# Modulation tiles of the first feed-forward stage in a ring of their own, and half-chunk steps

## The chip, the cores and the metric

The kernel runs on one core of one Trainium2 chip. The metric is the device time of one execution in microseconds (us); the median of three runs is given.

## The reference, cut to what matters

Two layers of a diffusion backbone work on two token streams of 256 tokens each (a latent and a context stream, D = 1024). Each layer is: a half-step SwiGLU feed-forward, a mixer of four branches (latent attention, Hyena convolution, S5 state space, neighbourhood attention), and a second half-step feed-forward. Each of these is wrapped in norms with shift, scale and gate vectors that come from the conditioning vectors:

```python
mod_l = (act_l @ w_mod[i] + b_mod[i])          # 9 vectors of 1024 for the latent stream
mod_c = (act_c @ w_mod[i][:, :n_c] + b_mod[i][:n_c])   # the same weights, context
def ffn_sublayer(x, mods, base, g_pre, g_post, w_in, w_out):
    h = rms_norm(x, g_pre) * (1 + mods[base + 1]) + mods[base]
    a, b = jnp.split(h @ w_in, 2, axis=-1)     # 1024 -> 2 x 2816
    return x + 0.5 * mods[base + 2] * rms_norm((silu(a) * b) @ w_out, g_post)
```

Vectors 0 to 2 belong to the first feed-forward, 3 to 5 to the mixer, 6 to 8 to the second feed-forward. The S5 parameters are turned into tables of powers, and the Hyena filters are computed by a small network with sines and a transform; neither depends on the tokens.

## The kernel before, in words

All large products run on TensorE (PE) in three passes of fp32r halves (hi x hi, hi x lo, lo x hi). A weight chunk of 128 x 1024 comes by a DMA of the SP queue into one of four slots of the tag `raw`, ACT makes its upper half `wh` (L220) and DVE its lower half `wl` (L221). The feed-forward (`ffn`) walks over 22 chunks f of 128 hidden columns; a chunk is two units (the a and the b half), each of 24 matmuls of 512 columns at full streams (L227 to L229, into one of four PSUM banks). `gate` forms silu(a) * b in a tile `t` (two slots) and splits it into `gg` (L541 to L548). The `gg` tiles of chunks 0 to 7, 8 to 15 and 16 to 21 lie in three pools. The output projection follows with 16 weight chunks, and then six more.

Side work is emitted in small steps. After each chunk `ffn` calls `step(2)`, and after each of the 16 weight chunks of the output projection `step(1)`. A `stepper` skips its first calls and then hands out tiles in proportion to the weights. A modulation tile (`mod_flow`, 128 x 1024 of `w_mod`, vector j, piece k) is summed with a fused DVE instruction for one stream (L328), and for the other by a product on GpSimd (POOL, L332) and a sum on ACT in the following step (L306). For layer 0 and j of 5 or more both streams are summed on DVE. For layer 1 and j of 5 or more there is one stream, and its pieces go to DVE and POOL in turn.

The first feed-forward of layer 0 (`ffn(0, 0, ...)`, called at L800) has three kinds of side work: the S5 setup (`setup_s5`, on POOL and DVE, emitted ahead of `ffn` with a lower priority; its memory is later that of the `gg` tiles of chunks 8 to 15, so these wait for its stores), the Hyena filters (`hyena_filters`, one step per call, closed at chunk 16), and vectors 2 to 8 of layer 0, whose tiles are loaded by SP into `raw` (L298). They begin after six calls. The second feed-forward of layer 0 (L815 to L832) computes vectors 0 to 4 of layer 1, and the first of layer 1 (called at L848) vectors 5 to 8; in these two the tiles have a ring of two slots, are loaded by POOL's queue, and POOL also computes S5 tables for layer 1 (`s5_tables` by way of `ahead`; PE transposes them at L1206 and multiplies them at L1217).

The order of PE's instructions is as written. On the other engines, and on the DMA queues, a planner with its own timeline sets the order when the program is built; `after(...)` puts an instruction behind a named one of the same engine.

Of the kernel before, what the change touches and what calls it, by code (L numbers as in the profile page):

```python
# [9 lines left out]
F32 = mybir.dt.float32  # L10
# [153 lines left out]
def build(tc, A):  # L164
# [20 lines left out]
    with st, tc.manual_schedule(engines={mybir.EngineType.PE}):  # L185
# [99 lines left out]
        def mod_flow(l, js, act, raw=None):  # L285

            if callable(act):
                act = act()  # L290
            tiles = [(j, k) for j in js for k in range(KT)]
            ws, back = {}, []

            def load(n):
                if n < len(tiles):
                    j, k = tiles[n]
                    ws[n] = raw() if raw else rp.tile([P, D], F32, tag="raw", name="raw")
                    (G.dma_start if raw else dma)(ws[n], A["wmod"][l, j, k])  # L298

            def finish():  # L300
                while back:
                    back.pop(0)()

            def sums(w, s, c):
                with after(mark["wh"]):
                    S.activation(w, w, AF.Copy, scale=0.5, accum_out=md[l][:, s, c : c + 1])  # L306

            def bias(j, ss):
                for s in ss:
                    m = md[l][:, s, j * KT : (j + 1) * KT]  # L310
                    V.tensor_tensor(m, m, bmt[l][:, j * KT : (j + 1) * KT], op=ALU.add)

            if raw:
                load(0)
                yield
            for n, (j, k) in enumerate(tiles):
                finish()
                load(n + 1 if raw else n)
                c = j * KT + k
                w = ws.pop(n)  # L320
                ss = [1] if l == 1 and j >= 5 else [0, 1]
                both = l == 0 and j >= JB
                fast = ss if both else [] if ss == [1] and k % 2 else [1]
                slow = [s for s in ss if s not in fast]
                for s in fast:
                    jk = sp.tile([P, D], BF16, tag="sq", name="jk", bufs=1)
                    with after(mark["wl"]):
                        V.scalar_tensor_tensor(  # L328
                            jk, w, 0.5, act[s], op0=ALU.mult, op1=ALU.mult, accum_out=md[l][:, s, c : c + 1]
                        )  # L330
                for s in slow:
                    G.tensor_tensor(w, w, act[s], op=ALU.mult)  # L332
                    back.append(lambda w=w, s=s, c=c: sums(w, s, c))
                if k == KT - 1:
                    back.append(lambda j=j, ss=ss: bias(j, ss))
                yield
            finish()

# [194 lines left out]
        def ffn(l, i, h, late, toks, nxt, gp, step, rows, fill, begun=(), xpool2=None):  # L533
            g = []
            begun = list(begun)
            cs_all = slice(min(toks) * P, NTOK)

            def new_unit(f, ab):
                return begun.pop(0) if begun else unit(l, i, h, f, ab, cs_all)

            def gate(f, ps):  # L541
                t = sp.tile([P, 512], F32, tag="t", name="t")
                S.activation(t[:, cs_all], ps[0][:, cs_all], AF.Tanh, scale=0.5)
                V.scalar_tensor_tensor(t[:, cs_all], t[:, cs_all], 1.0, ps[0][:, cs_all], op0=ALU.add, op1=ALU.mult)
                V.scalar_tensor_tensor(t[:, cs_all], t[:, cs_all], 0.5, ps[1][:, cs_all], op0=ALU.mult, op1=ALU.mult)
                gg = gp(f // 8).tile([P, 2, 512], F32R, tag="gg", name="gg", bufs=min(8, NF - f // 8 * 8))
                split(gg[:, 0, cs_all], gg[:, 1, cs_all], t[:, cs_all])
                g.append((gg[:, 0], gg[:, 1]))  # L548

            for f in range(NF):  # L550
                u = [new_unit(f, ab) for ab in range(2)]
                if late and f == 0:
                    u2 = [new_unit(1, ab) for ab in range(2)]
                    pss = []

                    def keep(v):
                        def run(cs):
                            ps = v(cs)
                            if cs is CTX:
                                pss.append(ps)  # L560
                                if len(pss) == 2:
                                    gate(0, pss)

                        return run

                    front([keep(u[0]), keep(u[1]), keep(u2[0])], late)
                elif late and f == 1:
                    gate(1, [pss[2], u2[1](None)])
                else:
                    gate(f, [v(None) for v in u])  # L570
                step(2)
                if f == NF - 3:
                    nxt["gr"] = rows()

            def lhs(kt, m):
                ms = slice(m * P, (m + 1) * P)
                return g[kt][0][:, ms], g[kt][1][:, ms]

            n_ = [0]

            def place():
                n_[0] += 1
                return gp((n_[0] - 1) // 8).tile([P, 2, 512], F32R, tag="gg", name="wf", bufs=8).rearrange("p a b -> p (a b)")

            fill()
            return outproj(lhs, NF, A["foa"][l, i], A["fob"][l, i], toks, nxt, xpool2 or (lambda: gp(3)), place, step)
# [18 lines left out]
        def ahead(stack, gp, name, slices):  # L605

            gp(0)
            gp(1)
            ts = ExitStack()
            tq = ts.enter_context(tc.tile_pool(name=name, bufs=1, reuse_waits="tile"))  # L610
            gen = s5_tables(E, L - 1, slices, tabd, sds, tq, lambda: psy.tile([P, 512], F32, tag="py", name="pn"))

            def close():
                for _ in gen:
                    pass
                ts.close()

            gp.before[2] = close
            f, n = [0], 4 * len(slices) + 3

            def go():
                f[0] += 1
                for _ in range(n * f[0] // 15 - n * (f[0] - 1) // 15):
                    next(gen, None)

            return go
# [35 lines left out]
        with ExitStack() as fs:  # L662
# [99 lines left out]
                    f()  # L762
            nxt = {}
            gp = Gates(fs, "A")
            gp(0)
            with ExitStack() as s1:
                tp5 = pool(s1, "s5s")
# [22 lines left out]
                        acts.extend(act_load())  # L790
                return acts

            st0 = stepper([(mod_flow(0, [2, 3, 4], acts0), 25), (mod_flow(0, [5, 6, 7, 8], acts0), 33)], 46, 6)

            def step0(w):
                st0(w)
                with after(mark["sp"], mark["dve"]):
                    next(hyg, None)

            late = ffn(0, 0, h, late, TALL, nxt, gp, step0, lambda: gate_rows(0, 0, 1, 0.5, [0, 1]), fill0, begun)  # L800
            h = nxt["h"]

        E = dict(locals())
        for l in range(L):
# [8 lines left out]
            with ExitStack() as fs:  # L813
# [4 lines left out]
                else:  # L818
# [3 lines left out]
                        n3.update(coeff=pre_coeff(1, 0, 0, [0, 1]), h=new_h())  # L822

                    x1, raw1 = mod_ring(fs, "mrB")
                    st1 = stepper([(mod_flow(1, [0, 1, 2, 3, 4], act_load, raw1), 42)], 50, 2)
                    tg1 = ahead(fs, gp, "s5p", range(0, 3))

                    def step1(w):
# [5 lines left out]
            if not last:  # L834
                with ExitStack() as fs:
# [4 lines left out]
                        n4.update(coeff=pre_coeff(1, 3, 2, [0, 1]), h=new_h())  # L840

                    x2, raw2 = mod_ring(fs, "mrC")
                    st2 = stepper([(mod_flow(1, [5, 6, 7, 8], act_load, raw2), 34)], 50, 2)
                    tg2 = ahead(fs, gp, "s5q", range(3, 8))

                    def step2(w):
# [44 lines left out]
def hyena_filters(tc, A, hp, psy, Hd, dma, cp, sp, rp, split):  # L891
# [12 lines left out]
    for l in range(L):  # L904
# [19 lines left out]
        for i, w in enumerate((w1, w2)):  # L924
            ps = psy.tile([P, 512], F32, tag="py", name="psm")
            T.matmul(ps[:64, :256], lhsT=w, rhs=cur, start=True, stop=True)
            a = hp.tile([64, 256], F32, tag="a", name="a")
            n = hp.tile([64, 256], F32, tag="n", name="n")
            V.tensor_scalar(
                a, ps[:64, :256], hv[:, 2 * i : 2 * i + 1], hv[:, 2 * i + 1 : 2 * i + 2], op0=ALU.add, op1=ALU.mult  # L930
            )
# [10 lines left out]
        for nt in range(2):  # L942
            f12 = []
            for j in range(2):
                ps = psy.tile([P, 512], F32, tag="py", name="psm")
                c = slice(nt * P, (nt + 1) * P)
                js = slice(j * 512, (j + 1) * 512)
                T.matmul(ps, lhsT=c2[:, c], rhs=w3[:, js], start=True, stop=False)
                T.matmul(ps, lhsT=c2[:, c], rhs=w3l[:, js], start=False, stop=True)
                f = hp.tile([P, 512], F32, tag="f12", name="f12", bufs=2)  # L950
                V.tensor_tensor(f, ps, dec[:, nt], op=ALU.mult)
                f12.append(f)
            pair = []
            for op in (ALU.add, ALU.subtract):
                su = hp.tile([P, 512], F32, tag="su", name="su", bufs=1)
                V.tensor_tensor(su, f12[0], f12[1], op=op)
                if nt == 0 and op == ALU.add:
                    V.tensor_tensor(su[0:1], su[0:1], hyd, op=ALU.add)
# [7 lines left out]
        for ri in range(2):  # L966
            for kt in range(2):
                ps = psy.tile([P, 512], F32, tag="py", name="psm")
                for nt in range(2):
                    c = slice(kt * P, (kt + 1) * P)  # L970
                    for i, (a, b) in enumerate(((0, 0), (0, 1), (1, 0))):
# [4 lines left out]
                            start=nt == 0 and i == 0,  # L976
                            stop=nt == 1 and i == 2,
                        )
                H = hp.tile([P, 512], F32, tag="f12", name="H", bufs=2)
                S.activation(H, ps, AF.Copy)  # L980
                dma(Hd[l][:, ri * 2 + kt], H)
            if ri == 0:
# [1252 lines left out]
```

## Time and profile before

| | us |
|---|---|
| median of three runs | 2654.64 (2652.17 to 2656.76) |
| the profiled execution | 2656.14 |
| its span | 2654.4 |
| PE busy in it | 2499.3 (94%) |
| DVE, ACT, POOL busy | 1719.9, 1096.1, 819.0 |

Times in the rows below are us from the start of the span unless marked ns. Engines: PE is TensorE's matmul, DVE VectorE, ACT ScalarE, POOL GpSimd, SP the engine that issues most DMAs; "SPq" is its queue. "L227" is line 227 of the kernel. PEclk is the granted TensorE clock as a share of full speed.

### The profile page before, as it was taken

The numbers are of one execution on the slowest core, as the hardware profiler recorded it, in microseconds if no ns is written. First come the engines' busy times: TensorE is split into PE (matmuls) and PEld (weight loads), VectorE is DVE, ScalarE is ACT, GpSimd is POOL, SyncE is SP. The second block draws the span as 40 slices with busy tenths as digits, with TensorE's granted clock in tenths as the row PEclk, the third lists the DMA queues.
The fourth block names the chain that finished last, engine by engine and source line by source line (L and its number), as shares of the span: only waits on it lengthen the run. The fifth ranks groups of instructions, "written<-read, shape, count | busy, mean of one in ns | idle before, by whom it ended". The sixth has DMA issues, their size and how long they took to land. (4 is left out here: it accounts for less than half of the span.)

```text
span 2654.4 us, 38042 instructions
## 1 busy us (share of the span) xinstructions
PE 2499.3 (94%) x14606; PEld 2107.5 (79%) x14606; DVE 1719.9 (65%) x2544; ACT 1096.1 (41%) x1860; POOL 819.0 (31%) x844
## 2 busy tenths in 40 slices
PE   6978999999999889999899998799999999998998
PEld 3856788987788767887778887677888989997997
DVE  6788995555645898556887546564535567776564
ACT  5435323454543232444444334333324555445443
POOL 4884000100102774006975406884201011100000
PEclk8989999999999999999999999999999999999999
DMA  6345675222232233344565544655542335776564
GB/s 238 104 151 197 214 249 195 84 75 84 74 111 71 85 94 104 94 166 161 179 194 185 205 142 141 198 185 187 175 158 76 92 100 189 282 247 212 160 191 143
DMA packets 134209, 411.06 MB, mean 155 GB/s; under 512 B 27095, under 2 KB 39176, under 8 KB 131212
## 3 DMA queue, kind: packets, MB, share of 16 engines
q1 hardware_dynamic: 117388, 349.33, 40.4%
q0 software_dynamic: 16640, 59.31, 6.4%
q8 instruction: 115, 1.88, 0.3%
q14 instruction: 66, 0.54, 0.1%
HBM read 374.41 MB, written 34.16 MB: 154 GB/s over the span
## 5 line engine op out<-in xcount | busy, mean ns | idle before, releaser
L221 DVE TENSOR_TENSOR wl<-raw,wh 128x1024 fp32r<-128x1024 f32 x424 | 565.3, 1334 | 537.0 <-ACT wh L220 529.8
L220 ACT ACTIVATE wh<-raw 128x1024 fp32r<-128x1024 f32 x424 | 449.2, 1060 | 846.9 <-issue 253.8
L227 PE MATMUL pin<-hh,wh 128*128 128x512 f32 (+1 forms) x1468 | 535.9, 365 | 20.3 <-ACT wh L220 12.4
L229 PE MATMUL pin<-hh,wl 128*128 128x512 f32 (+1 forms) x1468 | 531.5, 362 | 15.4 <-DVE wl L221 15.3
L228 PE MATMUL pin<-hl,wh 128*128 128x512 f32 (+1 forms) x1468 | 531.9, 362 | 1.7 <-DVE hl L415 1.6
L246 POOL TENSOR_TENSOR r<-v,mhalf 128x1 f32<-128x1 f32 (+2 forms) x46 | 30.7, 667 | 1015.2 <-DVE v L245 916.5
L227 PEld LDWEIGHTS pin<-hh,wh 128*128 128x128 f32 x1468 | 284.9, 194 | 66.8 <-ACT wh L220 15.3
L229 PEld LDWEIGHTS pin<-hh,wl 128*128 128x128 f32 x1468 | 284.2, 194 | 60.0 <-DVE wl L221 19.1
L228 PEld LDWEIGHTS pin<-hl,wh 128*128 128x128 f32 x1468 | 284.4, 194 | 43.2 <-DVE hl L415 3.3
L1322 PE MATMUL pm<-hh,wh 128*128 128x512 f32 (+1 forms) x704 | 251.3, 357 | 0.0
L1324 PE MATMUL pm<-hh,wl 128*128 128x512 f32 (+1 forms) x704 | 245.0, 348 | 0.2 <-DVE wl L221 0.2
L1323 PE MATMUL pm<-hl,wh 128*128 128x512 f32 (+1 forms) x704 | 244.9, 348 | 0.0
L458 PE MATMUL y<-wh,gg 128*128 128x512 f32 x448 | 177.2, 396 | 0.0
L459 PE MATMUL y<-wl,gg 128*128 128x512 f32 x448 | 177.2, 396 | 0.0
L460 PE MATMUL y<-wh,gg 128*128 128x512 f32 x448 | 177.2, 396 | 0.0
L332 POOL TENSOR_TENSOR mraw<-mraw,act 128x1024 f32<-128x1024 f32 x56 | 141.2, 2522 | 57.8 <-DMA mraw<-wmod 28.2
L1322 PEld LDWEIGHTS pm<-hh,wh 128*128 128x128 f32 x704 | 134.0, 190 | 18.1 <-issue 2.5
L1324 PEld LDWEIGHTS pm<-hh,wl 128*128 128x128 f32 x704 | 133.7, 190 | 17.8 <-DVE wl L221 0.4
L1323 PEld LDWEIGHTS pm<-hl,wh 128*128 128x128 f32 x704 | 134.0, 190 | 14.9
L328 DVE SCALAR_TENSOR_TENSOR jk<-raw,act 128x1024 bf16<-128x1024 f32 x88 | 119.8, 1361 | 3.6 <-DMA raw<-wmod 2.6
L1673 POOL TENSOR_TENSOR bt<-bt,mask 128x256 f32<-128x256 f32 x32 | 25.8, 837 | 267.0 <-DMA bt<-rpb 158.9
L227 PE MATMUL pm<-hh,wh 128*128 128x256 f32 (+1 forms) x320 | 103.5, 324 | 0.0
(488 smaller groups left out, 5112.0 us busy)
## 6 DMA issues: line engine op xcount, KB each, us to landing
raw<-fin SPq DMA_DIRECT2D x176, 512.0 KB, 3.7
raw<-winf SPq DMA_DIRECT2D x122, 512.0 KB, 3.5
mraw<-wmod POOLq DMA_DIRECT2D x72, 512.0 KB, 4.8
raw<-wmod SPq DMA_DIRECT2D x64, 512.0 KB, 4.5
raw<-foa SPq DMA_DIRECT2D x64, 512.0 KB, 3.6
raw<-wbr SPq DMA_DIRECT2D x32, 512.0 KB, 3.5
raw<-fob SPq DMA_DIRECT2D x24, 512.0 KB, 4.4
s5tabd<-rin POOLq DMA_DIRECT2D x8, 1152.0 KB, 5.3
```

Source lines behind the costliest of these rows:

```text
L220: mark["wh"] = S.activation(wh, w, AF.Copy)
L221: mark["wl"] = V.tensor_tensor(wl, w, wh.bitcast(F32), op=ALU.subtract)
L227: T.matmul(out, lhsT=lh, rhs=rh, start=first and i == 0, stop=False)
L228: T.matmul(out, lhsT=lh, rhs=rl, start=False, stop=False)
L229: T.matmul(out, lhsT=ll, rhs=rh, start=False, stop=last and i == n - 1)
L332: G.tensor_tensor(w, w, act[s], op=ALU.mult)
L458: T.matmul(o, lhsT=lh, rhs=rh, start=kt == 0, stop=False)
L459: T.matmul(o, lhsT=lh, rhs=rl, start=False, stop=False)
L460: T.matmul(o, lhsT=ll, rhs=rh, start=False, stop=kt == nk - 1)
L1322: T.matmul(o, lhsT=lh, rhs=rh, start=i == 0, stop=False)
L1323: T.matmul(o, lhsT=lh, rhs=rl, start=False, stop=False)
L1324: T.matmul(o, lhsT=ll, rhs=rh, start=False, stop=i == n - 1)
```

## The change

It has five parts. The tiles of the first feed-forward's vectors get a ring of two slots (`mod_ring`, "mrA"), are loaded by POOL's queue like those of the other two stages, and the ring's pool also serves the boundary rows (`xpool2`). In every ring the load of tile n + 1 is emitted behind the work on tile n, where it was ahead of it. The steps come after each unit instead of each chunk (`step(1)` twice in place of `step(2)`); skips, and the counters of the table and filter steps, follow. Vector 8 of layer 0 moves from the first to the second feed-forward of layer 0. The filters' scratch tiles (`a`, `n`, `f12`, `su`, `H`) take slots of the shared tags `h3` and `t` in place of their own.

```diff
@@ mod_flow
-                load(n + 1 if raw else n)
+                if not raw:
+                    load(n)
 ...
+                if raw:
+                    load(n + 1)
                 yield
@@ ffn
                     front([keep(u[0]), keep(u[1]), keep(u2[0])], late)
+                    step(1)
                 elif late and f == 1:
                     gate(1, [pss[2], u2[1](None)])
+                    step(1)
                 else:
-                    gate(f, [v(None) for v in u])
-                step(2)
+                    pa_ = u[0](None)
+                    step(1)
+                    gate(f, [pa_, u[1](None)])
+                step(1)
@@ ahead
-                for _ in range(n * f[0] // 15 - n * (f[0] - 1) // 15):
+                for _ in range(n * f[0] // 30 - n * (f[0] - 1) // 30):
@@ the first feed-forward of layer 0
             gp(0)
+            x0, raw0 = mod_ring(fs, "mrA")
...
-            st0 = stepper([(mod_flow(0, [2, 3, 4], acts0), 25), (mod_flow(0, [5, 6, 7, 8], acts0), 33)], 46, 6)
+            st0 = stepper([(mod_flow(0, [2, 3, 4, 5, 6, 7], acts0, raw0), 50)], 54, 4)
+            half = [0]
             def step0(w):
                 st0(w)
-                with after(mark["sp"], mark["dve"]):
-                    next(hyg, None)
+                half[0] += 1
+                if half[0] % 2 == 0:
+                    with after(mark["sp"], mark["dve"]):
+                        next(hyg, None)
-            late = ffn(0, 0, h, ..., fill0, begun)
+            late = ffn(0, 0, h, ..., fill0, begun, x0)
@@ the second feed-forward of layer 0
-                    st1 = stepper([(mod_flow(1, [0, 1, 2, 3, 4], act_load, raw1), 42)], 50, 2)
+                    acts1 = []
+                    def act1():
+                        acts1.extend(acts1 or act_load())
+                        return acts1[:2]
+                    st1 = stepper([(mod_flow(0, [8], act1, raw1), 10), (mod_flow(1, [0, 1, 2, 3, 4], act1, raw1), 42)], 54, 4)
@@ the first feed-forward of layer 1
-                    st2 = stepper([(mod_flow(1, [5, 6, 7, 8], act_load, raw2), 34)], 50, 2)
+                    st2 = stepper([(mod_flow(1, [5, 6, 7, 8], act_load, raw2), 34)], 50, 4)
@@ hyena_filters
-            a = hp.tile([64, 256], F32, tag="a", name="a")
-            n = hp.tile([64, 256], F32, tag="n", name="n")
+            a = sp.tile([P, 512], F32, tag="h3", name="a")[:64, :256]
+            n = sp.tile([P, 512], F32, tag="t", name="n")[:64, :256]
-                f = hp.tile([P, 512], F32, tag="f12", name="f12", bufs=2)
+                f = sp.tile([P, 512], F32, tag="h3", name="f12")
-                su = hp.tile([P, 512], F32, tag="su", name="su", bufs=1)
+                su = sp.tile([P, 512], F32, tag="t", name="su")
-                H = hp.tile([P, 512], F32, tag="f12", name="H", bufs=2)
+                H = sp.tile([P, 512], F32, tag="h3", name="H")
```

## Rows read from the trace of the kernel before

**Rows 1.** Windows by stage: length, busy us (and count) by engine, PEclk, DMA share, GB/s.

```profile
73.60:202.00 128.40, 108.38 (x449) 86.25 (x447) 102.15 (x196) 49.60 (x69) 109.10 (x121) 0.93 0.41 136
202.00:356.80 154.80, 146.91 (x611) 117.47 (x612) 141.06 (x194) 64.61 (x94) 37.77 (x13) 0.96 0.63 210
1217.00:1477.80 260.80, 248.76 (x1210) 206.42 (x1211) 201.18 (x221) 111.59 (x176) 185.27 (x162) 0.97 0.57 188
1617.00:1898.50 281.50, 256.74 (x1290) 211.78 (x1291) 165.15 (x192) 93.57 (x148) 176.91 (x207) 0.95 0.56 184
```

**Rows 2.** Timeline of PE, 79 to 158 us: start, length, instruction.

```profile
79.71 0.50 PE L227 MATMUL pin<-hh,wh 128*128 128x512 f32 x1
...
144.42 0.63 PE L227 MATMUL pin<-hh,wh 128*128 128x512 f32 x1
...
148.68 0.56 PE L228 MATMUL pin<-hl,wh 128*128 128x512 f32 x1
...
157.51 0.39 PE L227 MATMUL pin<-hh,wh 128*128 128x512 f32 x1
157.74 0.39 PE L228 MATMUL pin<-hl,wh 128*128 128x512 f32 x1
```

**Rows 3.** Waits of PE, 73.6 to 356.8 us: total us, times, longest; and one timeline row.

```profile
PE pin L229 <- DVE wl L221: 15.3, 6, 6.2
...
201.92 0.79 PE L227 MATMUL pin<-hh,wh 128*128 128x512 f32 x1 [9.50 <-ACT wh L220]
```

**Rows 4.** Waits of PE for tables: 1217 to 1477.8 us, then 1617 to 1898.5.

```profile
PE pn L1217 <- POOL vvt L1192: 7.9, 2, 6.5
...
PE pn L1206 <- POOL wt L210: 14.0, 3, 6.5
PE pn L1217 <- POOL vvt L1189: 8.4, 1, 8.4
```

**Rows 5.** Waits of the SP queue, 110 to 215 us, and one row of its timeline.

```profile
SPq L176 <- ACT raw L306: 38.7, 6, 13.4
...
189.78 4.75 SPq L176 DMA_DIRECT2D s5d<-s5tab  x8
```

**Rows 6.** POOL's window 89.87 to 189.65 us, all and L332 alone; POOL, DVE, ACT timeline.

```profile
89.87:189.65 99.78, 92.43 (x118) 0.93 0.33 106
89.87:189.65 99.78, 22.19 (x9) 0.93 0.33 106
131.93 2.40 POOL L332 TENSOR_TENSOR raw<-raw,act 128x1024 f32<-128x1024 f32 x1
131.97 3.44 DVE L328 SCALAR_TENSOR_TENSOR jk<-raw,act 128x1024 bf16<-128x1024 f32 x1
134.29 1.29 POOL L206 TENSOR_TENSOR s5pt<-s5ni 128x64 f32<-128x64 f32 x1
198.09 0.63 ACT L232 ACTIVATE gg<-t 128x512 fp32r<-128x512 f32 x1 [3.52 <-DMA s5d<-s5tab]
```

**Rows 7.** The loads of L298, 1200 to 1610 us: durations in ns, waits, landing.

```profile
L298 POOL DMA_DIRECT2D mraw<-wmod x42: 527/591/617, 1206.6 to 1591.5; - x42
  ACT mraw L306: 52.9, 23
DMA to landing us min/median/max: 3.7/4.7/6.5
```

**Rows 8.** Window 1236 to 1290 us: L332 alone, all engines, L328 alone.

```profile
1236.00:1290.00 54.00, 17.26 (x7) 1.00 0.58 189
1236.00:1290.00 54.00, 54.00 (x270) 44.52 (x269) 45.83 (x50) 23.47 (x37) 41.20 (x41) 1.00 0.58 189
1236.00:1290.00 54.00, 8.86 (x14) 1.00 0.58 189
```

**Rows 9.** A wait of POOL, 1617 to 1800 us, and the window of that stretch.

```profile
POOL mraw L332 <- DMA mraw<-wmod: 5.7, 3, 3.1
...
1617.00:1800.00 183.00, 158.24 (x831) 130.65 (x832) 110.03 (x132) 60.30 (x98) 145.65 (x177) 0.92 0.55 180
```

More of the change, by code (lines that the diff above doesn't have):

```diff
@@ L791, in acts0 @@
                 return acts
-            st0 = stepper([(mod_flow(0, [2, 3, 4], acts0), 25), (mod_flow(0, [5, 6, 7, 8], acts0), 33)], 46, 6)
+            st0 = stepper([(mod_flow(0, [2, 3, 4, 5, 6, 7], acts0, raw0), 50)], 54, 4)
+            half = [0]
             def step0(w):
                 st0(w)
-                with after(mark["sp"], mark["dve"]):
-                    next(hyg, None)
-            late = ffn(0, 0, h, late, TALL, nxt, gp, step0, lambda: gate_rows(0, 0, 1, 0.5, [0, 1]), fill0, begun)
+                half[0] += 1
+                if half[0] % 2 == 0:
+                    with after(mark["sp"], mark["dve"]):
+                        next(hyg, None)
+            late = ffn(0, 0, h, late, TALL, nxt, gp, step0, lambda: gate_rows(0, 0, 1, 0.5, [0, 1]), fill0, begun, x0)
             h = nxt["h"]
```

## The prediction, made before the changed kernel ran

> **What bounds the kernel now.** I read the engine shares first (PE busy 94% of the span, so only its gaps and slow stretches can be won back), then busy time by stage, then who PE waits for in each stage, then the queues behind those waits. The change touches three feed-forward stages; call them A (layer 0, first), B (layer 0, second) and C (layer 1, first). In each the chunk phase (22 chunks f of two units, before the output projection) is where PE falls short [rows 1]. A's phase, 73.6 to 356.8 us, holds 449 + 611 = 1060 matmuls. At full clock one starts 0.227 us after the other, at the lower of the two levels (1.2 against 2.4 GHz) 0.426 us: eleven start between 144.42 and 148.68 [rows 2], so A's floor is 1060 x 0.2267 = 240 us, and 283 us are used: 28 us are idle and the granted clock (0.93 and 0.96) accounts for 128.4 x 0.07 + 154.8 x 0.04 = 15 us. B loses 12 us idle in tables and C 25 us, with clocks of 0.97 and 0.95 (8 and 14 us). These eleven stand right behind PE's gap of 6.2 us [rows 3], so such a gap costs 11 x 0.2 = 2 us more than its length.
>
> Who ends the waits differs. In A it is the weights' halves, wl and wh [rows 3]; in B and C it is POOL's tables for S5 [rows 4]. In A two causes lie behind wl and wh. The SP queue feeds weights and modulation tiles through the same four "raw" slots, and 38.7 us of its waits before 215 us are for ACT to finish a modulation tile [rows 5]: weights queue behind a slot that a slow tile holds. And S5's setup ends at 189.7 us; its stores sit on SP ahead of the next weights from 189.78 for 4.75 us, and gg of chunk 8, whose slots lie on the setup's memory, starts at 198.09 [rows 5, 6]. PE's longest gap, 9.5 us, ends at 201.92 with chunk 10 [rows 3]. So until 202 us the setup is a second chain beside PE, and not later than it by much: with no losses PE would stand at the end of chunk 9 at about 175 us (chunk 2 starts at 79.7 [rows 2]; 8 x 48 x 0.2267 = 87 us, and some 8 us of filter matmuls).
>
> **The change, part by part.**
>
> *Modulation tiles of A leave "raw" for two slots of their own and are loaded by POOL.* The 48 SP loads and the waits for ACT before them go; SP carries weights (and the filters' loads) alone. That takes away the gaps that come from the ring. Between 202 and 356.8 us, where nothing else holds PE, they are 154.8 - 146.9 = 8 us and, at a clock of 0.96, 6 us more [rows 1]; I let 3 us of these 14 stand.
>
> *But the tiles now start at chunk 2, not at chunk 6* (four half-chunk steps are skipped where six whole ones were), and each puts a load on POOL as well as its product. POOL does S5's setup at that time: from 89.87 to 189.65 us it is busy 92.4 us, 22.2 of them nine products, so 70.2 us belong to the setup and 7.4 are idle [rows 6]. The order there shows that a product goes in whenever it is ready: at 131.93 a product, at 134.29 the setup again. A load costs POOL 0.59 us [rows 7]. With n tiles before its end the setup ends at 89.9 + 70.2 + 7.4 + n x (2.47 + 0.59) = 167.5 + 3.06 n; with nine loadless products this gives the 189.7 of the trace. One tile per unit (5.44 us, rate 0.93) from chunk 2 on, and PE can go on to the end of chunk 11 (two t slots hold chunks 8 and 9, the four PSUM tiles chunks 10 and 11): n is 10 if the planner lets the setup go first for some time, 18 to 20 if it does not. I take 19: the end is 225.6 us, 36 us later. PE resumes 12.2 us behind it as before (189.7 to 201.9), at 238. I let it have stopped one unit short of that limit: 5 us, ten more chunks of 48 x 0.2267 (109 us), 8 us of the filters' second layer, 2 us of low clock behind the long gap and the 3 us left above end the phase at 365 instead of 356.8. **A: +8 us**, ends -38 (setup not held up, floor plus 5 us) and +37 (below).
>
> *Load behind the product instead of ahead of it, and steps after each unit* (all three stages). The wait of a load for ACT's sum, 52.9 us over B's 42 loads [rows 7], no longer holds up the product behind it. Two tiles in one step, where the second's load has just been issued and lands 4.7 us later, become one per 5.4 us. In C, while the tables are made, products wait 5.7 us for such loads, and POOL is then the bound: busy 145.7 of 183 us, with PE's clock at 0.92 [rows 9]. I take 5 of the 5.7 off PE's 25 us of idle time, and 2 of clock. **C: -7 us**, ends -36 (the 25 idle and most of the 14 of clock) and +10 (the tables' steps come up to half a chunk earlier, and PE meets them sooner: once more the longest gap, 8.4, and its 2 us of clock).
>
> *Vector 8 of layer 0 moves to B.* Eight tiles with two DVE sums each and no POOL product come first there. In 1236 to 1290 POOL makes seven products (17.3 us) and DVE seven sums (8.9 us); these seven products go, so the tables that PE meets at chunks 7 and 8 are early: the 6.5 us gap goes, and of the 5.5 us that are left half, 2.7 (POOL enters the last slice of tables with less behind it). With 3 us of clock that is 12 us off. DVE pays: some 17.6 sums of 1.27 us, 22.3, in place of 8.9 in 54 us, where it is busy 45.8 [rows 8]: 59 us, over by 5, if its own instructions stay as long. They get shorter where POOL makes no product (the sum at 131.97, beside one, took 3.44 us [rows 6]), and two units of wl are ahead of PE, so I count 2 us. **B: -10 us**, ends -16 and +12 (the 5 us of excess, the clock behind it, and a table gap that stays). In A the eight tiles lay in the output projection, where PE never waited: nothing is won.
>
> *Filter scratch in shared tags.* The same instructions; `t` and `h3` have two slots each. A gate holds its `t` for one unit and a half, so a second is free for the filters, except while chunks 8 and 9 wait for gg: that lies inside the wait counted above. 0 us, at most the 2 us of one DVE chain twice. The boundary rows of A share the ring, as B's and C's did: the last tile ends some 3 steps (16 us) before they are loaded: 0. The step counters that are doubled with the step rate (30 for 15) place the tables' steps at the same chunks: 0.
>
> Sum: 2656.1 (this execution; its span and 1.7 around it) + 8 - 10 - 7 = 2647. The execution lies 1.5 us above the median of the three runs.
>
> The Trainium skill ("SBUF — State Buffer", the box on DVE blocking DMA) says that a transfer issued by GpSimd has its descriptors written by that engine's cores, which VectorE can shut out of their common port, so that it appears slow; it names 620 ns against 3100. By the rows such loads landed 3.7 to 6.5 us after issue in B, with DVE busy 77% of it [rows 7, 1], so no such delay is seen for these forms of DVE work. By the rule each of A's loads could come 2.5 us later (an estimate from that page).
>
> **Rivals.** *1, slower: the setup is pushed out of reach.* Place: POOL, 85 to 250 us of A. Twenty tiles at 3.06 us, and per tile 1.3 us of waiting for ACT (52.9 / 42) with the setup queued behind: end 167.5 + 20 x 4.3 = 254, PE resumes at 266 and the phase ends at 394, +37. With B and C at -17 that is 2676; without their gain 2693. It decides from where the setup ends later than some 235 us (then A's loss exceeds B's and C's gain). For it: two-slot loads waited so in B; against it: the load now stands behind the product, when the sum is mostly done.
> *2: the setup keeps its place.* If its instructions go ahead of the tiles, n is 0 to 8, PE passes chunk 11 without a wait, A's phase is 245 to 258 us, -25 to -38. 2656 - 30 - 17 = 2609. For it: after its first product the trace has setup and products in turn, not products alone [rows 6]; against: products cut in as soon as there were any.
> *3: the waits change their names only.* POOL stays the bound of the tables in B and C, and A gains after 202 what it loses before: 2651 to 2661.
> *4: loads by POOL land late under DVE's work.* At the slowest landing of the rows, 6.5 + 0.6 us against a step of 5.4, DVE waits 1.7 us on each of 37 tiles, 63 us in a phase where it is busy 243 of 283: some 20 us reach PE, 2671. The median landing of 4.7 speaks against it. The Trainium skill's page named above speaks for it.
>
> **How the numbers follow.** Forecast 0.45, rival 1 0.19, rival 2 0.2, rival 3 0.12, rival 4 0.04. About 0.2% (5 us) is what a measurement here tells from no change. The forecast's own range is 2633 to 2660; of it four fifths are faster, the rest the same: faster 0.36 + 0.2 = 0.56; the same 0.09 + 0.08 = 0.17; slower 0.19 + 0.04 + 0.04 = 0.27. The range for 8 in 10 reaches into rivals 1 and 2: 2606 to 2676.
>
> **What would show it.** SP's waits for ACT's modulation sums gone from A; POOL's last setup instruction at 215 to 235 us, and one long gap of PE that ends some 12 us behind it, with chunk 10 to 12; hardly a gap after it; B's gap at chunk 8 gone, and C's table gaps down by a third. Wrong would make it: a setup that ends before 200 us (rival 2) or after 235 (rival 1); DVE waiting for tiles that POOL loaded (4); gaps in B before 1290 us, from DVE.

## The result: 1.4% slower, and where the time went

The changed kernel takes 2692.72 us (median of 4 runs, 2691.61 to 2693.62) against 2655.13 for the kernel before on the same chip (4 runs): a ratio of 1.0136, 95% interval 1.0124 to 1.0149. The forecast was 2647 with a range of 2606 to 2676. Both were wrong; the time lies beside rival 1's 2693, though only a part of rival 1's mechanism stands behind it.

The profiled executions span 2654.4 and 2689.8 us. Cut at the first matmul into pin and the first into y of each feed-forward, the spans compare so (us):

| stage | before | after | difference |
|---|---|---|---|
| A: chunk phase | 306.0 | 328.4 | +22.4 |
| A: output projection | 123.9 | 123.9 | 0 |
| mixer of layer 0 | 723.2 | 724.2 | +1.0 |
| B: chunk phase | 273.9 | 268.3 | -5.6 |
| B: output projection | 123.8 | 135.9 | +12.1 |
| C: chunk phase | 296.6 | 299.7 | +3.1 |
| C: output projection | 123.8 | 123.8 | 0 |
| mixer of layer 1 | 431.7 | 429.4 | -2.3 |
| last feed-forward | 191.4 | 191.3 | -0.1 |
| start of the last matmul to the end of the span | 9.0 | 13.9 | +4.9 |

With 0.1 us less ahead of A they add up to the 35.4 us between the spans. Stages of the same code differ by some 4 us between the 14 traces of this document (the mixer of layer 1 takes 429.4 to 433.2 us), so rows of 3 us and less say little by themselves. The forecast had +8, -10 and -7 for A, B and C and nothing anywhere else.

**A.** The windows of the kernel after (columns as in [rows 1]): A up to the end of its longest gap and from there to the output projection; B's chunk phase without its first matmuls; B's output projection; C's chunk phase, cut like B's.

```profile
73.60:259.20 185.60, 134.19 (x544) 105.39 (x542) 143.53 (x238) 71.08 (x104) 152.78 (x152) 0.88 0.45 147
259.20:379.10 119.90, 119.90 (x515) 98.12 (x516) 90.32 (x141) 41.68 (x59) 16.75 (x20) 0.98 0.55 176
1240.30:1495.45 255.15, 247.64 (x1209) 205.16 (x1210) 206.70 (x236) 102.10 (x160) 173.27 (x155) 0.98 0.58 189
1495.50:1631.40 135.90, 128.28 (x544) 102.34 (x543) 76.39 (x101) 55.44 (x93) 52.12 (x39) 0.97 0.56 183
1647.00:1931.40 284.40, 258.43 (x1290) 212.96 (x1291) 180.22 (x191) 93.67 (x148) 175.75 (x207) 0.94 0.54 182
```

PE's waits in A, after:

```profile
PE psm L944 <- ACT cur L953: 32.7, 1, 32.7
PE pin L229 <- DVE wl L221: 14.4, 7, 3.9
PE pin L227 <- DVE t L547: 4.2, 1, 4.2
```

Behind 259 us PE is busy 119.90 of 119.90 us at a clock of 0.98: no time is idle there any more, where before 8 us were idle and the clock was 0.96 [rows 1]. The waits for wh are gone, and so are SP's for ACT's modulation tiles [rows 3, 5]. All of the loss and more is one gap. 515 matmuls follow it, 10 chunks of 48 and 35 of the filters, so PE stopped at the end of chunk 11. How the gap ends, in rows of five engines, ordered by engine and not by time (start, length, instruction):

```profile
241.03 0.35 POOL L210 TENSOR_TENSOR s5ni<-s5ni,s5pt 128x64 f32<-128x64 f32 x1
...
219.50 20.81 SPq L176 DMA_DIRECT2D raw<-fin  x4
240.79 6.30 SPq L176 DMA_DIRECT2D s5d<-s5tab  x8
...
251.79 1.15 ACT L232 ACTIVATE gg<-t 128x512 fp32r<-128x512 f32 x2 [5.56 <-DMA s5d<-s5tab]
258.70 0.42 ACT L953 ACTIVATE cur<-a 64x256 f32<-64x256 f32 x1
...
253.66 0.28 DVE L902 TENSOR_SCALAR n<-a 64x256 f32<-64x256 f32 x1
...
259.17 1.11 PE L944 MATMUL psm<-cur,w 64*64 64x256 f32 x2 [32.75 <-ACT cur L953]
```

It is the chain of [rows 6], only later: the setup's last instruction at 241.4 us instead of 189.7, the stores, gg of chunks 8 and 9 at 251.8 instead of 198.1. The releaser that the profile names, cur, is the last link only. The filter's vector n could not be written until a gate gave back its t slot, and both gates that held one stood waiting for gg.

**B and C.** The gap at chunk 8 of B is gone as forecast: 247.64 of 255.15 us are busy, and no wait in that phase for tables is left but one of 5.3 us, at chunk 13, where it was 1.4 before. But the output projection, in which PE had no wait before, now has waits for wl of 7.5 us and a clock of 0.97 instead of 1.00. Its window in the kernel before:

```profile
1477.80:1601.60 123.80, 123.80 (x544) 100.66 (x543) 55.06 (x79) 46.77 (x77) 25.06 (x25) 1.00 0.48 161
```

C's table waits are 25.9 us (24.7 before).

### The profile page after: what moved, and what is told of

The parts are those of the page before. It is cut to its first block, busy times and chain, and to the rows that moved or that the text cites. A ratio compares the mean times of both kernels' runs of the same rounds, so it can differ in the third digit from the quotient of the medians.

```text
span 2689.8 us, 38047 instructions
## 1 busy us (share of the span) xinstructions
PE 2502.2 (93%) x14606; PEld 2108.7 (78%) x14606; DVE 1738.1 (65%) x2544; ACT 1093.5 (41%) x1858; POOL 857.6 (32%) x900
## 3 DMA queue, kind: packets, MB, share of 16 engines
q0 software_dynamic: 24704, 88.67, 10.0%
## 5 line engine op out<-in xcount | busy, mean ns | idle before, releaser
L221 DVE TENSOR_TENSOR wl<-raw,wh 128x1024 fp32r<-128x1024 f32 x424 | 583.3, 1376 | 505.2 <-ACT wh L220 498.4
L333 POOL TENSOR_TENSOR mraw<-mraw,act 128x1024 f32<-128x1024 f32 x80 | 211.3, 2642 | 117.6 <-DVE jk L329 85.8
L329 DVE SCALAR_TENSOR_TENSOR jk<-mraw,act 128x1024 bf16<-128x1024 f32 x144 | 199.1, 1383 | 48.9 <-DMA mraw<-wmod 48.6
L306 ACT ACTIVATE mraw<-mraw 128x1024 f32<-128x1024 f32 x80 | 84.4, 1055 | 179.4 <-POOL mraw L333 179.4
L298 POOL DMA_DIRECT2D mraw<-wmod x128 | 72.1, 563 | 261.5 <-DVE jk L329 125.7
```

What stands on the lines that cost most here:

```text
L221: mark["wl"] = V.tensor_tensor(wl, w, wh.bitcast(F32), op=ALU.subtract)
```

## The experiments

Five rounds each. Ratios are to the kernel before, run beside them; "chunk phase" is meant as in the table.

**1. The filter's n out of the shared slot**

```
-            n = sp.tile([P, 512], F32, tag="t", name="n")[:64, :256]
+            n = sp.tile([P, 512], F32, tag="sq", name="n", bufs=1)[:64, :256]
```

> The changed kernel, but the filter scratch vector n (64 x 256) lies in the one-slot tag of VectorE's throw-away sums (jk) instead of in t; only VectorE writes either, so n waits for no gate any more. The planned order of POOL has 15 products ahead of the last S5 setup instruction instead of 19. Theory 1 (PE's 32.7 us gap in A is the late setup; the shared slot adds only the 3.6 us by which PE resumes later behind gg than before, 7.4 against 3.8 us): the setup ends 4 x 3.06 = 12 us earlier, at about 229; PE's gap still begins at the end of chunk 11, is called a wait for the gate (pin), and ends near 243: gap 16 to 18 us, the kernel 14 to 18 us faster than the changed one, about 2677. Theory 2 (the shared slot is the cause: without it PE would not stand at chunk 11): no gap above 10 us, A's phase ends near 350, about 2662.

Measured: 2675.66 us, ratio 1.0067 (1.0054 to 1.0080), 17 us under the changed kernel. Sixteen products run ahead of the setup's end, which comes at 224.86; PE stops at the same chunk, and its gap has the gate's name:

```profile
223.65 1.21 POOL L210 TENSOR_TENSOR s5ni<-s5ni,s5pt 128x64 f32<-128x64 f32 x1
...
238.69 0.79 PE L227 MATMUL pin<-hh,wh 128*128 128x512 f32 x1 [18.41 <-DVE t L547]
```

Without the shared slot PE stands all the same, so the slot is not the cause. What it costs is seen behind gg: PE resumes 4.2 us after gg (234.45) here, 3.8 before [rows 3, 6], 7.4 in the changed kernel. So it cost 3 to 4 us there. The edit also changed the planned order (16 products for 19), and with it the setup ends 16.5 us earlier. Together they make A's chunk phase 21 us shorter (307.3); B's output projection (137.9) and C's chunk phase (302.3) give back 2 and 3.

**2. A's tiles later, all behind the setup**

```
-            st0 = stepper([(mod_flow(0, [2, 3, 4, 5, 6, 7], acts0, raw0), 50)], 54, 4)
+            st0 = stepper([(mod_flow(0, [2, 3, 4, 5, 6, 7], acts0, raw0), 50)], 42, 18)
```

> The changed kernel, but A's modulation tiles start at chunk 9 (18 half-chunk steps skipped instead of 4, the rate raised from 50/54 to 50/42), so that no product and no load of them lies ahead of the S5 setup on POOL. Theory 1: the setup ends before 180 us, PE's gap of 32.7 us and the one before it go, and A's phase ends between 335 and 350 instead of 379: 2650 to 2665. Theory 2 (shared filter scratch holds PE): a wait of the filter's second matmul of over 10 us stays although the setup is early, above 2675.

Measured: 2657.32 us, ratio 1.0005 (0.9996 to 1.0015): A's loss is gone, with the shared scratch as it was. The setup's last instruction in POOL's timeline, and PE's waits in A (to 339.3 us):

```profile
153.41 0.35 POOL L210 TENSOR_TENSOR s5ni<-s5ni,s5pt 128x64 f32<-128x64 f32 x1
```

```profile
PE pin L229 <- DVE wl L221: 14.7, 7, 5.1
PE pin L227 <- ACT wh L220: 0.2, 1, 0.2
```

A's chunk phase takes 288.8 us, 40 less than in the changed kernel. Its output projection, which gets more tiles, takes 129.4. Theory 1 holds.

**3. The loads of A's tiles back on SP, the early start and the slots kept**

```
-                    (G.dma_start if raw else dma)(ws[n], A["wmod"][l, j, k])
+                    (G.dma_start if raw and (l or j == 8) else dma)(ws[n], A["wmod"][l, j, k])
```

> The changed kernel with the loads of A's modulation tiles issued by SP again; two slots of their own, the early start and everything else stay. The planned order has some 16 products ahead of the setup's end instead of 19. Theory 1 (products and loads on POOL are what delays the setup): 18 loads of 0.59 us and 3 products of 2.5 us go, the setup ends near 223 instead of 241.4 and PE's gap of 32.7 us shrinks by 15 to 19; 2673 to 2678. Rival (SP, which waits for ACT's sums with weights queued behind, pays it back): waits of PE for wl and wh above 25 us, 2684 to 2695.

Measured: 2672.19 us, ratio 1.0065 (1.0051 to 1.0079), 0.8 under theory 1's range, which had no term for the end of the program (4.2 us shorter here). The setup ends at 218.1 with 17 products and no load ahead of its end, and the gap is

```profile
242.62 1.11 PE L944 MATMUL psm<-cur,w 64*64 64x256 f32 x2 [14.74 <-ACT cur L953]
```

SP does wait 69.1 us for ACT's sums, but PE's waits for wl and wh in A's chunk phase are 18.2 us, against 14.4 in the changed kernel and 27.7 before, and the time is under the rival's 2684: the rival falls.

**4. and 5. B and C alone: first without, then with the moved vector.** Both have A of the kernel before, with its tiles in raw and the filter scratch in its own tags; the last two lines of this diff, against the changed kernel, are bc_only's alone.

```
-                st0(w)
                 half[0] += 1
                 if half[0] % 2 == 0:
+                    st0(2 * w)
...
-  st1 = stepper([(mod_flow(0, [8], act1, raw1), 10), (mod_flow(1, [0, 1, 2, 3, 4], act1, raw1), 42)], 54, 4)
+  st1 = stepper([(mod_flow(1, [0, 1, 2, 3, 4], act1, raw1), 42)], 50, 4)
```

> The kernel before, with the change in B and C only and without the moved vector: loads behind their products, one step after each unit; A, its scratch and vector 8 as before. Theory 1 (A holds all of the loss but some 7 us; the moved vector's VectorE work costs B its 6.7 us): B gains 3 to 8 us, C stays within 3: 2645 to 2655. Rival (the half-chunk steps and the later loads themselves cost in B and C): 2660 to 2668.

> As bc_only, with vector 8 of layer 0 moved to B, so B and C are those of the changed kernel; A is that of the kernel before with eight tiles fewer in its output projection. Theory 1: A's loss of 22 us is gone and B and C cost what they do in the changed kernel, 6.7 + 3: 2660 to 2668. Rival (B and C lose only because A hands over late work): equal to the kernel before within 3 us.

Measured: bc_only 2663.54 us, 1.0025 (1.0014 to 1.0036); bc_v8 2658.92, 1.0006 (0.9997 to 1.0015). The first is a miss for theory 1: load order and half-chunk steps by themselves cost B's chunk phase 4.2 us and C's 6.8. The second lies where the rival had it, within 3 us of the kernel before, but not for the rival's reason: with the vector, B's chunk phase is at 270.1 (-3.8) and its output projection at 132.5 (+8.7), so the pattern of the changed kernel shows without its A; the 9.4 us that A's chunk phase is shorter there, with eight tiles fewer, hide it in the total. In bc_only the output projection takes 123.9.

**6. and 7. Half-chunk steps alone, load order alone** (each the kernel before with that part of the diff)

> The kernel before with one step after each unit in B and C (the tables' steps and the tiles' at half chunks), loads ahead of products and vector 8 in A as before. bc_only, which has the loads behind as well, made B's chunk phase 278.1 us (273.9 before) and C's 303.4 (296.6). Theory 1 (the steps that come half a chunk earlier meet PE sooner: this is where the loss is): B and C lose 8 us or more, 2662 to 2666. Theory 2 (the load order costs it): both within 2 us of before, 2655 to 2658.

> The kernel before with the load behind the product in B and C and nothing else. Theory 1 (half-chunk steps are the cause): within 3 us of the kernel before, 2653 to 2659. Theory 2 (the load order is): 2661 to 2667.

Measured: half_only 2661.39 us, 1.0010 (1.0001 to 1.0019); order_only 2660.15, 1.0009 (1.0000 to 1.0018). Neither theory as stated: by the medians they cost 2.9 and 1.7 us (by the intervals 0.3 to 5.0 and 0 to 4.8), and together 7 (3.7 to 9.6, run 4). B's chunk phase is 277.7 and 277.6 (+3.8, +3.7); C's is 301.7 with the half steps (+5.1) and 298.4 with the order (+1.8). The profiled execution of half_only is 5.5 us above its median, so its stages can overstate the cost. B's output projection takes 123.9 in both. PE's waits for tables in C (1606.5 to 1908.2 us) with half steps, against [rows 4]:

```profile
PE pn L1220 <- POOL wt L210: 14.0, 3, 6.0
PE pn L1231 <- POOL vvt L1203: 10.2, 1, 10.2
PE pn L1231 <- POOL vvt L1206: 2.1, 1, 2.1
PE pn L1220 <- POOL wt L207: 2.0, 1, 2.0
```

The longest grew from 8.4 to 10.2 and one for wt from 0.2 to 2.0.

**8. Load first again, vector 8 in B, half steps** (bc_v8 with the load ahead of the product)

> As bc_v8 (A of the kernel before, vector 8 in B, one step after each unit), but the load stands ahead of the product again. In bc_v8 B's output projection took 132.5 us instead of 123.9: VectorE waits there 11.6 us for tiles that have not landed, with wl queued behind. Theory 1 (the load behind the product makes tiles late where two come in one step): these waits shrink below 4 us and the output projection is back at 124 to 126; 2652 to 2655. Theory 2 (it is the number of tiles left for that stretch, 14 products instead of 7): it stays above 130 us, 2657 to 2662.

Measured: 2658.41 us, 1.0002 (0.9993 to 1.0011); the output projection takes 132.8. The load order is not what costs there. That spoke for the number of tiles, until the next run.

**9. The changed kernel with one step per chunk in B and C**

```
                     def step1(w):
-                        st1(w)
-                        tg1()
+                        h1[0] += 1
+                        if h1[0] % 2 == 0:
+                            st1(2 * w)
+                            tg1()
...
```

(The dots stand for the same in C, and for the skips and the tables' counters, which go back to those of the kernel before. The wrapper also acts in the output projections: two tiles after every second weight chunk there, in place of one after each.)

> The changed kernel with one step per chunk in B and C (the wrapper steps every second time with twice the weight, so the tiles of B's output projection are the same in number); A unchanged. Theory 1 (B's output projection loses 12 us because with one step per unit its tiles run in pairs, two products and then two loads, so that VectorE waits for both tiles with wl behind it; and C loses 3 to 5 because its tables' steps come earlier): B's output projection goes from 135.9 to 124 to 126, C's chunk phase to 296 to 299, 2674 to 2682. Theory 2 (eight more tiles in B are the cause, however they are stepped): 2688 to 2694.

Measured: 2683.26 us, 1.0102 (1.0089 to 1.0115), some 9 us under the changed kernel and 1 us over theory 1's range. B's output projection is back at 123.9 us and C's chunk phase at 296.5 (296.6 before), with the vector still in B. So the number of tiles alone is not what costs there. Nor are the steps alone: runs 4 and 6 have them without the vector, and 123.9 us. It takes both: the six kernels here with half-chunk steps and the vector in B have 132.5 to 137.9 us in that stretch, the other eight 123.8 or 123.9. What both together do there, in POOL's timeline of the changed kernel:

```profile
1501.73 3.32 POOL L333 TENSOR_TENSOR mraw<-mraw,act 128x1024 f32<-128x1024 f32 x1 [1.17 <-DVE jk L329]
1504.98 0.59 POOL L298 DMA_DIRECT2D mraw<-wmod  x1
1506.53 0.53 POOL L298 DMA_DIRECT2D mraw<-wmod  x1 [0.96 <-ACT mraw L306]
1510.58 2.77 POOL L333 TENSOR_TENSOR mraw<-mraw,act 128x1024 f32<-128x1024 f32 x1 [3.52 <-DVE jk L329]
1514.53 3.32 POOL L333 TENSOR_TENSOR mraw<-mraw,act 128x1024 f32<-128x1024 f32 x1 [1.17 <-DVE jk L329]
```

and with 13 tiles in that stretch but two to a step (run 10):

```profile
1502.01 0.59 POOL L298 DMA_DIRECT2D mraw<-wmod  x1 [2.05 <-ACT mraw L306]
1503.17 2.39 POOL L332 TENSOR_TENSOR mraw<-mraw,act 128x1024 f32<-128x1024 f32 x1 [0.57 <-DVE jk L328]
1507.61 0.59 POOL L298 DMA_DIRECT2D mraw<-wmod  x1 [2.05 <-ACT mraw L306]
1508.77 2.39 POOL L332 TENSOR_TENSOR mraw<-mraw,act 128x1024 f32<-128x1024 f32 x1 [0.57 <-DVE jk L328]
```

and with half-chunk steps but without the vector (half_only), five products in that stretch:

```profile
1496.29 0.59 POOL L298 DMA_DIRECT2D mraw<-wmod  x1 [7.55 <-ACT mraw L306]
1497.45 2.40 POOL L332 TENSOR_TENSOR mraw<-mraw,act 128x1024 f32<-128x1024 f32 x1 [0.57 <-DVE jk L328]
1501.85 0.59 POOL L298 DMA_DIRECT2D mraw<-wmod  x1 [2.00 <-ACT mraw L306]
1503.00 2.39 POOL L332 TENSOR_TENSOR mraw<-mraw,act 128x1024 f32<-128x1024 f32 x1 [0.57 <-DVE jk L328]
```

In the first, two products and then two loads: both slots are empty at once, and VectorE, whose sum comes before the product, waits for both. In the other two a load is on its way while the other tile is worked on. All six of those kernels have the pairs, also v8_load_first, whose loads are emitted ahead of the products; none of the others has. Why the planner falls into pairs there is not shown. VectorE's waits for tiles in that stretch, and PE's behind them, changed kernel (first two rows), then run 10:

```profile
DVE jk L329 <- DMA mraw<-wmod: 13.7, 14, 2.1
...
PE y L462 <- DVE wl L221: 7.5, 4, 3.0
```

```profile
DVE jk L328 <- DMA mraw<-wmod: 0.5, 2, 0.3
```

**10. to 12. Versions to beat both.** best1: the changed kernel with A's tiles from chunk 7 (steps 44, 14), loads ahead of products, and one step per chunk in B and C as in run 9. best2: the same from chunk 9 (42, 18). best3: best1 with run 3's loads on SP.

> A combination: in A the two own slots, loads by POOL and half-chunk steps of the change, but the tiles start at chunk 7 (14 half-chunk steps skipped, rate 50/44); loads ahead of products; in B and C one step per chunk as before, with vector 8 in B. By theory 1 the setup has POOL to itself until about 150 us: A's chunk phase is 12 to 17 us shorter than before (306.0), its output projection 0 to 5 longer, B and C within 5, the end of the program 5 longer: 2640 to 2652. If the tiles that are left for the output projections of A and B hold PE, 2655 to 2662.

> best1 with A's tiles starting at chunk 9 (18 half-chunk steps skipped, rate 50/42). The setup is early in both, so it decides only how the 48 tiles are spread. late_start had A's chunk phase at 288.8 and its output projection at 129.4, together 418.2; best1 has 296.5 + 123.8 = 420.3. If the later start pays in the chunk phase and the tiles are not paired with load ahead: 2643 to 2649. If the output projection loses its 5 us again: 2649 to 2653, the same as best1.

> best1 with the loads of A's 48 tiles issued by SP instead of POOL. From the last store's issue to the end of the span it was 5.6 us in the kernel before, 10.4 in the changed one; over the runs so far the stretch behind the last matmul goes with the packets of the software queue: 9.0 us with 16640, 9.7 to 10.0 with 17792, 13.9 to 14.0 with 24704. Theory 1 (that queue's use sets it): 17792 packets and 9.7 to 10.0 us here, A within 3 us of best1: 2644 to 2649. Rival (the stretch goes with the code of A's ring, not with the queue; SP's waits for ACT's sums hold the weights): 13.9 us stays, or A loses more than 4: 2650 to 2656.

Measured: best1 2650.76 us, 0.9970 (0.9960 to 0.9980); best2 2648.88, 0.9969 (0.9959 to 0.9979), the same, as its output projection in A takes 127.5; best3 2640.74, 0.9947 (0.9934 to 0.9960), 15 us under the kernel before. In best3 A's chunk phase takes 289.3 us, and B's output projection 123.9. It beat its forecast of 2644 to 2649: A was to be within 3 us of best1's 296.5 and is 7 shorter. In best1 A's gain fell short of its 12 to 17 us: 9.6. Four products run ahead of the setup's end in both; it comes at 174.8 in best1, with four loads, and at 165.7 in best3, with none.

## Why the prediction was wrong

**The step that failed in A is the price of a tile.** "The setup ends at 89.9 + 70.2 + 7.4 + n x (2.47 + 0.59) = 167.5 + 3.06 n": n was 19, as taken, but the end is 241.4, not 225.6. Run 2 has the end with no tile ahead of it: 153.8, not 167.5. From there the kernel before shows (189.7 - 153.8) / 9 = 4.0 us for each of its nine products, and the changed kernel 87.6 / 19 = 4.6 with the load, run 1 (224.9 - 153.8) / 16 = 4.4, run 3 without loads (218.1 - 153.8) / 17 = 3.8. Where a tile's cost lies is read from the window of that chain, from its first to its last instruction: run 2, with no tile in it, then the changed kernel, there POOL alone in the last two rows (L333, L298) and one wait:

```profile
89.64:153.76 64.12, 59.00 (x257) 47.70 (x256) 44.12 (x104) 20.05 (x25) 58.02 (x109) 0.98 0.23 68
```

```profile
98.98:241.38 142.40, 108.78 (x432) 84.92 (x431) 110.56 (x163) 52.56 (x79) 126.14 (x144) 0.90 0.43 137
98.98:241.38 142.40, 42.86 (x17) 0.90 0.43 137
98.98:241.38 142.40, 10.66 (x18) 0.90 0.43 137
POOL mraw L333 <- DVE jk L329: 11.7, 6, 2.5
```

The same 109 instructions, all but one the setup's, take POOL 58.0 us with no tile among them, 92.4 - 22.2 = 70.2 in the kernel before [rows 6], and 126.1 - 42.9 - 10.7 = 72.6 in the changed kernel. So 12 of the 70.2 us that my formula took for fixed had come with the nine tiles: with the products' 22.2 they are nearly all of the 35.9 us between the two ends. From run 2 to the changed kernel the 87.6 us are 42.9 of products, 10.7 of loads, 14.6 by which the setup's own instructions are longer, 10.1 more of idle time (POOL waits 11.7 us for VectorE's sums ahead of products, with the setup behind them) and 9.3 by which the chain starts later, with two products and a load ahead of it. What lengthens the setup's instructions no run separates. The longest stands, in the changed kernel, beside VectorE instructions without a pause; the same instruction later:

```profile
145.05 5.59 POOL L208 TENSOR_TENSOR s5ni<-s5nr,s5ni 128x64 f32<-128x64 f32 x1
...
154.40 0.32 POOL L208 TENSOR_TENSOR s5ni<-s5nr,s5ni 128x64 f32<-128x64 f32 x1
```

My formula was fitted to one point, nine products; it reproduced that point because base and slope were off by amounts that cancel there. With the end of run 2, the price of the kernel before (4.0) and the load of [rows 7] (0.6), one gets 153.8 + 19 x 4.6 = 241. The price is not a constant, though: the four tiles of best1 cost 5.2 us each, those of best3, without loads, 3.0.

**The 12.2 us from the setup to PE were 17.8.** Of these 5.6 us more, 3.6 are the step "Filter scratch in shared tags. [...] 0 us": its cover was right (the slots are held only while gg waits), but inside that wait it puts a vector chain and a table load behind the gate and ahead of PE. The other 2 pass between the setup's end and gg, where the stores took 6.30 us on SP instead of 4.75.

**PE's place was right**: "PE can go on to the end of chunk 11". With 10 chunks left instead of 10 and a half, and 3 instead of the 5 us that I had left for losses and clock, the remainder took 120 us where I had 127. So the phase came out 14 us over the forecast, with PE's return 21 us over it.

**B: the forecast of the chunk phase had the right mechanism** and half the size (-5.6 for -10): the gap of 6.5 us went, but of the rest a later wait grew from 1.4 to 5.3 us where I had 2.7 left. What failed is "In A the eight tiles lay in the output projection, where PE never waited: nothing is won". It is wrong for A: without the vector A's chunk phase is 7.8 us shorter in run 5 than in run 4, and 8.8 in run 8 than in run 6, with 8 products ahead of the setup's end for 9. And I never went on to ask where B's tiles would then lie: 14 of 48 fall into B's output projection. There the step "Two tiles in one step [...] become one per 5.4 us", which I took for a gain, together with the vector turned alternating loads into pairs (run 9) and cost 12.1.

**C: "-7" was +3.1**, a sign that stood only in the bounds ("the tables' steps come up to half a chunk earlier, and PE meets them sooner"). Runs 6 and 9 show it, and all traces together: the chunk phase of C takes 296.5 to 299.8 us in the six kernels with one step per chunk (mean 297.8) and 298.7 to 303.4 in the eight with half-chunk steps (300.6). The load behind the product won nothing that PE could use: with one step per chunk it gives 296.5 (run 9) and 298.4 (run 7). Whether the costs of runs 6 and 7 simply add up to the 7 us of run 4 is not settled; the intervals allow it.

**The end of the program** had no term in the sum at all, and cost 4.9 us (last section).

**The rivals.** Rival 1's outcome is what happened in A, a setup pushed past its deciding point of 235 us, at 4.6 us a tile (4.3 there) and +22 us instead of +37. Its reason held only in part: the waits for ACT that it charged at 1.3 us a tile came to 0.3 us in the whole window of the setup, and the terms above stand in their place. That the total equals its 2693 is chance: the other 13 us are in the main the net of B's output projection, C and the end of the program, which no rival had, and of B's gain. Rival 4's waits of VectorE for tiles came, but not for its reason: the loads of B's output projection landed after 3.7 to 5.7 us, median 4.1, sooner than in [rows 7]. In A, where the rival had 63 us of such waits, there are 15.2, with landings of 3.6 to 8.3 us, median 4.3. So the delay of which the Trainium skill warns ("SBUF — State Buffer", the box on DVE blocking DMA) is not seen there either.

## What to carry to other kernels

When a stage shares an engine with a second chain, the price of one more guest instruction is not its duration: the guests also lengthen the chain's own instructions, hold it in waits and start it later. Measure the price from two points of the chain's end, not from one, one of them with no guest at all, and keep the guests out until the chain is through; here a later start alone took back the whole loss (run 2). A step that feeds a two-slot ring must keep one load in flight while the other tile is in use: look at the timeline for load, product, load, product, and follow moved work into the stage in which it ends up, also where that stage had no wait before.

## What the runs showed of the hardware

The stretch from PE's last matmul to the end of the span goes with the traffic of the queue that POOL's loads use. Its rows, before, after, and best3:

```profile
q0 software_dynamic: 16640, 59.31, 6.4%
```

```profile
q0 software_dynamic: 24704, 88.67, 10.0%
```

```profile
q0 software_dynamic: 17792, 63.50, 6.9%
```

Over the 14 kernels profiled here, 16640 packets go with 9.0 us, 17792 with 9.7 to 10.0 and 24704 with 13.9, whatever else was changed: 4.9 us for 8064 packets, or 0.09 for each load of 144. The instructions at the end are the same; from the issue of the last stores the wait is simply longer (5.6 us before, 10.4 after). best3's number was forecast in this way before it ran. By what it is spent the trace does not show.
